# Hybrid streaming encoder step on one core: the residual rows' scaling and the first operand set of the lower product are put beside the second pair of up-projections

## The chip, the cores and the metric

One core of a Trainium2 chip runs the whole step as one program. The metric is device microseconds of that program. Five engines matter: TensorE (PE, with its weight loads as PEld), VectorE (DVE), ScalarE (ACT), GpSimd (POOL) and SyncE (SP), which issues the transfers. Each engine runs its own instructions strictly in the order in which they were written out, and waits by semaphores for the others' data.

## What is computed

The reference is one layer of an encoder over 640 tokens (512 prompt, 128 sample), width 1024: attention and a convolution branch, a merge, then a feed-forward part, a gated embedding and a norm. The part that the change touches is the feed-forward part:

```
x = x + (gate_a * attn_branch + gate_c * conv_branch) @ w_out
x = x + square(relu(rmsnorm(x, norm_ffn_g) @ w_ff_up)) @ w_ff_down     # 1024 -> 4096 -> 1024
x = x + sigmoid(rmsnorm(x, ple_norm_g) @ w_ple_gate) * (p_emb @ w_ple_proj)
```

The norm's factor r per token is not applied before the up-projection. With y = square(relu((x*g) @ w_up)) the product gives y*r*r, so the kernel multiplies the residual rows x by the row `vrow` = 1/(r*r) = mean(x*x) + eps instead, adds y @ w_down to that, and lets the later norms take the factor out. The eight residual rows (128 channels x 640 tokens each) must therefore have been multiplied by `vrow` before the first result of the lower product is added to them.

## The kernel before, in words

All products keep full precision by splitting every operand into a high and a low part (high by ACT, low = value - high by DVE or POOL) and adding three matmuls. The feed-forward products use a seven-product scheme on 2x2 blocks, so each operand is first turned into seven combinations.

- `up(n)`, n = 0..15, is one block of the up-projection: four operand tiles A, B, C, D are prepared from two weight slabs `raw_up{n}a/b` (sums `S` at L1854, L1858, L1862, L1865; high parts L1839; low parts L1846), then seven products M1, M5, M6, M3, M7, M2, M4 of 12 matmuls each (L1918) go in that order into the PSUM banks a, b, a, b, a, c, a. `times` appends every product to the list `chain`. Sums of banks are L1957 and L1940; relu and square are L1978 to L1984. For even n the sums S lie in PSUM, for odd n in SBUF, made by POOL.
- Two blocks, up(2c) and up(2c+1), make a pair; their squared results y lie in one buffer `staged[c]`. There is one slot "y" for it in the plan: the first square of a pair (Z12 of the even block, which also gives back bank b) takes the slot, and the last low part of `convert(c)` gives it back. There are five banks "q" for the products.
- `convert(c)` makes the seven operands of the lower product from `staged[c]`: three differences on POOL and one on DVE (L2079), seven high parts on ACT (L2047), six low parts on DVE and one on POOL (L2054, all named f).
- `down(c)` is the lower product: four groups j of weights (`raw_down`, L2114 to L2141), each seven products of 6 matmuls (L2185) whose results DVE adds to the residual rows (L2222).
- `start_row(m)`, m = 0..7, multiplies residual row m by `vrow` on POOL (L1817). The addition L2222 to row m waits for it.

The order on each engine is made before the launch by a planner (`Plan`): every step is given an engine, an estimated cost, the steps that it depends on and a due key; the planner repeatedly takes the step with the least start + 0.01 x key. Steps that are listed as dependencies only shape this order; on the chip an instruction waits for its data alone. Slots of weight pairs ("w", three), raw slabs ("r", three), banks and ring tiles are granted in that plan too. In the plan before, `start_row` has the keys T_0 + 20 + 2m and depends on `vrow`, and `convert(0)` the key T_0 + 17.8, ahead of the products of up(2) (T_0 + 22.8) and up(3) (T_0 + 34.2). T_0 is the due key of the first up-projection.

Of the kernel before, what the change touches and what calls it, by code (L numbers as in the profile page):

```python
# [62 lines left out]
SQ2, START, SQ3 = "POOL", "POOL", "POOL"  # L63
# [8 lines left out]
FAST = (0, 1, 2, 3, 4, 5, 6)  # L72
# [27 lines left out]
class Plan:  # L100
# [7 lines left out]
    def op(self, eng, cost, fn, deps, key, get="", put=""):  # L108
        if eng == "DVE2":
            eng, port = "DVE", True  # L110
        else:
            port = eng == "POOL"
        self.port.append(port and LOCK > 0)
        self.ops.append((eng, cost, fn, [d if isinstance(d, tuple) else (d, self.wait) for d in deps], key, get, put))
        return len(self.ops) - 1
# [53 lines left out]
def encoder_step_kernel(ctx: ExitStack, tc: tile.TileContext, a: dict, o: dict):  # L169
# [597 lines left out]
    for m in range(4):  # L767
        ps = product(f"qn{m}", blocks(slab(), range(6)), cq, ntaps=QN_TAPS[m])
        for j in range(2):
# [5 lines left out]
                op=ALU.mult,  # L775
# [132 lines left out]
    for j in range(4):  # L908
# [3 lines left out]
        for i in range(2):  # L912
            m = 2 * j + i
# [13 lines left out]
    op = plan.op  # L927
# [57 lines left out]
    for m in range(4):  # L985
# [21 lines left out]
        c = op("PE", 1.3, kn, ukd, -20 + m, get="p")  # L1007
# [6 lines left out]
    for t in range(4):  # L1014
# [18 lines left out]
        c = op("PE", 1.3, vn, uvd, -16 + t, get="p")  # L1033
# [28 lines left out]
    for g in range(2):  # L1062
        k_, wkb, wkd = slab_op(-19, raw_only=True)
        for ct in range(2):
# [21 lines left out]
            c = op("PE", 0.87, qn, wkd, -19, get=QB)  # L1086
# [353 lines left out]
    op = plan.op  # L1440
# [38 lines left out]
    def token_row(i, out, dep, key):  # L1479

        bx = {}

        def diagonal():
            bx["dg"] = ring(f"dg_{i}")
            nc.vector.tensor_tensor(
                out=bx["dg"].rearrange("p (t n) -> p t n", t=NT),
                in0=ident[:, None, :].to_broadcast([P, NT, P]),
                in1=one[i][:, :, None].to_broadcast([P, NT, P]),
                op=ALU.mult,
            )  # L1490

        def spread():
            bx["b"] = [qbank(f"psb_{i}{s}") for s in range(2)]
            for s in range(2):
                nc.tensor.matmul(bx["b"][s][:, :HT], ones, bx["dg"][:, s * HT : (s + 1) * HT], start=True, stop=True)
            plan.give(bx["dg"])

        def copy():
            t = out()
            for s in range(2):  # L1500
                nc.scalar.activation(t[:, s * HT : (s + 1) * HT], bx["b"][s][:, :HT], AF.Copy)
            plan.give(*bx["b"])

        d1 = op("DVE2", 0.73, diagonal, [dep], key, get="t")
        d2 = op("PE", 0.6, spread, [d1], key, get="qq", put="t")
        return op("ACT", 0.7, copy, [d2], key, put="qq")
# [39 lines left out]
    chain = []  # L1546
# [121 lines left out]
    grid, sq_done, xr_done, readers = {}, [], {}, {}  # L1668
# [130 lines left out]
    T_0 = 6.5 * 4  # L1799
# [11 lines left out]
    a3 = token_row("v", lambda: vrow, a2, T_0 + 10)  # L1811
    squared = op("DVE", 0.1, v_squared, [a2], T_0 + 20)
    started = []

    def start_row(m):
        def go():
            engines[START].tensor_tensor(out=x2[m], in0=x2[m], in1=vrow, op=ALU.mult)  # L1817

        started.append(
            op(START, 1.5 if START == "POOL" else 0.73, go, [a3, (started or [a3])[-1]] + readers[m], T_0 + 20 + 2 * m)  # L1820
        )

    for m in range(8):
        start_row(m)

    staged, opened = {}, {}

# [537 lines left out]
    key, fdone = T_0, {}  # L2365

    def ups(c, key):
        fdone[c] = up(2 * c, key) + up(2 * c + 1, key + T_UP)
# [1 line left out]
    ups(0, key)  # L2370
    key += 2 * T_UP
    for c in range(8):
        opnds = (convert if c in FAST else plain_convert)(c, key - 5 if c == 0 else key, fdone[c])
        if c < 7:
            ups(c + 1, key)
            key += 2 * T_UP
        used.clear()
        (down if c in FAST else plain_down)(c, key, opnds)
        key += T_DN if c in FAST else 26.0
# [414 lines left out]
```

## Time and profile before

| | |
|---|---|
| median of three runs | 1003.73 us (997.35, 1003.73, 1003.88) |
| the profiled execution | 998.67 us |
| its span, first to last instruction | 996.8 us |
| PE busy | 968.8 us (97%) |
| DVE busy | 797.5 us (80%) |
| ACT, POOL busy | 506.4 us (51%), 371.4 us (37%) |
| chain that ended last | PE 88%, DVE 8%, ACT 2% |

Times are microseconds from the span's start. A busy PE is not PE at its peak: at the lower granted clock a matmul lasts longer and still counts as busy. In a timeline, a row gives start, duration, engine, line, operation, result and operands, and in brackets how long the engine had been idle before it and who ended that.

### The profile page before, as it was taken

The page shows a single profiled execution, that of the slowest core. Times are in us where ns is not written, and L with a number is a line of the kernel's source. Part 1 is how long each engine was busy: PE and PEld are TensorE (multiplying, and loading weights), DVE is VectorE, ACT ScalarE, POOL GpSimd, SP SyncE. Part 2 cuts the span into 40 slices and gives each one's busy share as a digit, 9 for nine tenths or more (in the row PEclk, how much of TensorE's full clock was granted, in tenths as well). Part 3 has the DMA queues.
Part 4 walks back from the last instruction along what each step waited for, and adds up shares of the span by engine and source line. Part 5 has one row for each costly group of instructions (what it writes and reads, how often), then busy time and mean ns, then how long its engine had stood idle before and what let it go on. Part 6 is the DMA issues. An engine that isn't in the chain of part 4 may idle for free.

```text
span 996.8 us, 17051 instructions
## 1 busy us (share of the span) xinstructions
PE 968.8 (97%) x6576; PEld 935.2 (94%) x6576; DVE 797.5 (80%) x1415; ACT 506.4 (51%) x939; POOL 371.4 (37%) x270
## 2 busy tenths in 40 slices
PE   9999999999999899999998999999999999999995
PEld 8999989999999667799998999999999999999995
DVE  7596899995554887687779999999999999996445
ACT  7344644223443687635665455555555555645442
POOL 0354559322201443001239435354545454323111
PEclk9999999999999999999998899999999999999998
DMA  6329213312242433414221132322222222342203
GB/s 234 117 81 96 96 49 101 117 64 85 64 132 71 136 105 115 131 44 143 86 72 56 64 89 84 98 83 93 85 86 85 85 85 85 112 128 64 86 1 106
DMA packets 34705, 92.53 MB, mean 93 GB/s; under 512 B 8800, under 2 KB 11488, under 8 KB 34624
## 3 DMA queue, kind: packets, MB, share of 16 engines
q1 hardware_dynamic: 34480, 91.42, 30.5%
q8 instruction: 52, 0.85, 0.3%
q14 instruction: 29, 0.24, 0.1%
q10 hardware_dynamic: 144, 0.03, 0.0%
HBM read 86.12 MB, written 3.91 MB: 90 GB/s over the span
## 4 chain that ended last, share of the span: by engine, by line
PE 88%; DVE 8%; ACT 2%; issue 1%; DMA 1%; POOL 0%; SPq 0%; DVEq 0%; POOLq 0%; ACTq 0%
PE a L1918 11%; PE da L2185 9%; PE sa L342 6%; PE sc L342 6%; PE wo L1687 6%; PE b L1918 5%; PE db L2185 5%; PE pg L2481 3%; PE ao L1624 3%; PE co L342 3%; PE pd L2301 3%; PE c L1918 3%; PE glu_b L342 2%; PE glu_a L342 2%; PE dc L2185 2%; PE pg L2557 2%
## 5 line engine op out<-in xcount | busy, mean ns | idle before, releaser
L2141 POOL TENSOR_TENSOR lo_B<-raw_down,hi_B 128x768 fp32r<-128x768 f32 x28 | 51.8, 1850 | 44.5 <-PE da L2185 24.4
L485 DVE SCALAR_TENSOR_TENSOR cv<-uP,keep,cv 128x512 f32<-128x512 f32 x87 | 65.6, 754 | 2.4
L2222 DVE TENSOR_TENSOR x<-da,x 128x320 f32<-128x320 f32 x112 | 53.8, 485 | 3.1 <-PE da L2185 0.9
L510 POOL TENSOR_TENSOR acc<-acc,tap 128x640 f32<-128x640 f32 x30 | 49.2, 1639 | 10.1 <-ACT tap L502 8.7
L2185 PE MATMUL da<-f,hi_B 128*128 128x320 f32 x224 | 50.2, 310 | 0.0
L2185 PE MATMUL da<-f,hi_A 128*128 128x320 f32 x224 | 49.5, 307 | 0.0
L2185 PE MATMUL db<-f,hi_A 128*128 128x320 f32 x224 | 49.5, 307 | 0.0
L1714 POOL TENSOR_TENSOR ssum<-ssum,sq 128x640 f32<-128x640 f32 x7 | 11.1, 1592 | 90.5 <-ACT sq L1711 90.5
L2122 POOL TENSOR_TENSOR raw_down<-raw_down 128x256 f32<-128x256 f32 x28 | 21.4, 764 | 61.2 <-DVE S L2114 60.8
L2134 ACT ACTIVATE hi_B<-raw_down 128x768 fp32r<-128x768 f32 x28 | 23.8, 848 | 31.5 <-PE a L1918 13.3
L1687 PE MATMUL wo<-mgl,hi_wo 128*128 128x320 f32 x128 | 39.4, 308 | 0.0
L1687 PE MATMUL wo<-mgh,hi_wo 128*128 128x320 f32 x128 | 39.1, 305 | 0.0
L1687 PE MATMUL wo<-mgh,lo_wo 128*128 128x320 f32 x128 | 39.0, 305 | 0.0
L2185 PEld LDWEIGHTS da<-f,hi_B 128*128 128x128 f32 x224 | 36.9, 187 | 0.7 <-DVE x L2222 0.2
L2185 PEld LDWEIGHTS db<-f,hi_A 128*128 128x128 f32 x224 | 37.1, 187 | 0.0
L2185 PEld LDWEIGHTS da<-f,hi_A 128*128 128x128 f32 x224 | 37.1, 187 | 0.0
L2134 ACT ACTIVATE hi_A<-S 128x512 fp32r<-128x512 f32 (+1 forms) x56 | 26.8, 479 | 17.4 <-DVE S L2128 17.4
L2185 PE MATMUL da<-f,lo_A 128*128 128x320 f32 x112 | 34.4, 307 | 0.8 <-DVE lo_A L2141 0.7
L2185 PE MATMUL da<-f,lo_B 128*128 128x320 f32 x112 | 34.2, 305 | 0.0
L2185 PE MATMUL db<-f,lo_A 128*128 128x320 f32 x112 | 34.2, 305 | 0.0
L2054 POOL TENSOR_TENSOR f<-y,f 128x640 fp32r<-128x640 f32 x7 | 11.7, 1675 | 59.7 <-ACT f L2047 59.7
L485 DVE SCALAR_TENSOR_TENSOR cv<-uS,keep,cv 128x128 f32<-128x128 f32 x87 | 31.0, 356 | 3.2
(684 smaller groups left out, 3770.6 us busy)
## 6 DMA issues: line engine op xcount, KB each, us to landing
raw_down<-in_w_down_dram SPq DMA_DIRECT2D x32, 512.0 KB, 3.7
raw_w_gate<-in_w_gate_dram SPq DMA_DIRECT2D x16, 512.0 KB, 3.5
raw_cache_T<-in_cache_T_dram SPq DMA_DIRECT2D x8, 512.0 KB, 3.8
raw_cache_V<-in_cache_V_dram SPq DMA_DIRECT2D x8, 512.0 KB, 3.5
raw_wo<-in_w_out_dram SPq DMA_DIRECT2D x8, 512.0 KB, 3.6
raw_pg<-in_w_pg_dram SPq DMA_DIRECT2D x8, 512.0 KB, 3.6
raw_w_glu<-in_w_glu_dram SPq DMA_DIRECT2D x6, 512.0 KB, 4.4
raw_w_cq<-in_w_cq_dram SPq DMA_DIRECT2D x6, 512.0 KB, 3.7
```

The costliest lines, as they stand in the source:

```text
L342: nc.tensor.matmul(ps[:m, s, :HT], w_, x_[:, s * HT : (s + 1) * HT], start=st_, stop=sp)
L485: nc.vector.scalar_tensor_tensor(out=outs[i] if j == W - 1 else sums[i], in0=src, scalar=wj, in1=sums[i], op0=ALU.mult, op1=ALU.add,)
L510: nc.gpsimd.tensor_tensor(out=acc[:, 0, :], in0=acc[:, 0, :], in1=t, op=ALU.add)
L1624: nc.tensor.matmul(ps[:, :HT], w_, x_[:, halves_[s]], start=k == 0 and n == 0, stop=k == 3 and n == 2)
L1687: nc.tensor.matmul(bx[s][:, :HT], w_, x_[:, n_], start=k == 0 and j == 0, stop=k == 7 and j == 2)
L1918: nc.tensor.matmul(bx[bank][:, :HT], w_, x_, start=first and k == 0 and i == 0, stop=k == 3 and i == 2, skip_group_check=True,)
L2134: nc.scalar.activation(bx[tile][0][:, dst], src(), AF.Identity)
L2141: eng.tensor_tensor(out=l_, in0=src(), in1=h_.bitcast(F32), op=ALU.subtract)
L2185: nc.tensor.matmul(bx[bank][:, :HT], w_, x_, start=first and n == 0 and i == 0, stop=n == 1 and i == 2, skip_group_check=True,)
L2222: nc.vector.tensor_tensor(out=d, in0=bx[bank][:, :HT], in1=d, op=ALU.add)
L2301: nc.tensor.matmul(ps[:, :HT], w_, x_, start=b_ == 0 and q_ == 0, stop=b_ == 3 and q_ == 2)
L2481: nc.tensor.matmul(bx[s][:, :HT], w_, x_[:, n_], start=k == 0 and i == 0, stop=k == 7 and i == 2)
```

## The change

`start_row` gets a gate. Row m additionally depends, in the plan, on one product of the second pair: `chain[n_ + 5 + m]`, where `n_` is the length of `chain` before up(2) was added, so the gates are M2 and M4 of up(2) and then M1, M5, M6, M3, M7, M2 of up(3). Its key moves from T_0 + 20 + 2m to T_0 + 60 + 2m. The eight rows are no longer created right after `vrow` but after up(2) and up(3). `convert(0)` is created there too: its key moves from T_0 + 17.8 to T_0 + 45.6, and it additionally depends on `chain[n_ + 1]`, which is M5 of up(2). The other seven calls of the conversion keep their keys and dependencies.

```
-    def start_row(m):
+    def start_row(m, gate_):
...
         started.append(
-            op(START, 1.5 if START == "POOL" else 0.73, go, [a3, (started or [a3])[-1]] + readers[m], T_0 + 20 + 2 * m)
+            op(
+                START,
+                1.5 if START == "POOL" else 0.73,
+                go,
+                [a3, (started or [a3])[-1], gate_] + readers[m],
+                T_0 + 60 + 2 * m,
+            )
         )
-
-    for m in range(8):
-        start_row(m)
...
     for c in range(8):
-        opnds = (convert if c in FAST else plain_convert)(c, key - 5 if c == 0 else key, fdone[c])
+        if c:
+            opnds = (convert if c in FAST else plain_convert)(c, key, fdone[c])
         if c < 7:
+            n_ = len(chain)
             ups(c + 1, key)
             key += 2 * T_UP
+            if c == 0:
+
+                opnds = convert(c, key, fdone[c] + [chain[n_ + 1]])
+                for m in range(8):
+                    start_row(m, chain[n_ + 5 + m])
```

## Rows read from the trace of the kernel before

**Rows 1.** Stretches, all engines: the first feed-forward stretch and the first later cycle, columns named

```profile
core 0: us, PE busy (x) PEld busy (x) DVE busy (x) ACT busy (x) POOL busy (x), PEclk, DMA share, GB/s
503.00:588.35 85.35, 79.47 (x510) 76.86 (x509) 75.42 (x121) 43.73 (x90) 51.06 (x32) 0.94 0.24 75
588.35:637.23 48.88, 48.88 (x339) 48.70 (x338) 46.22 (x90) 26.77 (x54) 23.17 (x16) 1.00 0.28 87
```

**Rows 2.** The first of those stretches, matmuls of L1918, then of L2185

```profile
503.00:588.35 85.35, 54.63 (x338) 52.48 (x339) 0.94 0.24 75
...
503.00:588.35 85.35, 23.52 (x156) 22.69 (x156) 0.94 0.24 75
```

**Rows 3.** Stretches of ten microseconds inside the first stretch, same columns as rows 1

```profile
530.00:540.00 10.00, 10.00 (x71) 9.94 (x69) 8.88 (x9) 5.78 (x12) 10.00 (x6) 1.00 0.17 53
540.00:550.00 10.00, 6.04 (x25) 5.38 (x25) 10.00 (x8) 3.87 (x6) 10.00 (x6) 0.65 0.16 52
550.00:560.00 10.00, 8.91 (x48) 8.04 (x47) 8.44 (x15) 5.67 (x14) 1.26 (x2) 0.84 0.22 68
```

**Rows 4.** Timeline of PE: matmuls after a wait, and two at the lower clock

```profile
542.16 0.41 PE L1918 MATMUL a<-h2t34h,hi_D 128*128 128x320 f32 x1 [1.89 <-DVE y L1940]
...
543.48 0.47 PE L1918 MATMUL a<-h2t34l,hi_D 128*128 128x320 f32 x1
543.75 0.47 PE L1918 MATMUL a<-h2t34h,lo_D 128*128 128x320 f32 x1
...
547.62 0.63 PE L1918 MATMUL a<-h2b,lo_A 128*128 128x320 f32 x1 [2.07 <-DVE lo_A L1846]
```

**Rows 5.** Chain that ended last, in order of time: start, length, what

```profile
560.70 1.73 PE c L1918 x12
...
564.17 0.88 PE da L2185 x6
```

**Rows 6.** Timeline of POOL: the residual rows and what is queued behind them

```profile
526.37 6.62 POOL L1817 TENSOR_TENSOR x<-x,vrow 128x640 f32<-128x640 f32 x4
532.94 2.03 POOL L2079 TENSOR_TENSOR T<-y 128x640 f32<-128x640 f32 x1
534.93 4.13 POOL L1817 TENSOR_TENSOR x<-x,vrow 128x640 f32<-128x640 f32 x2
539.02 2.00 POOL L2079 TENSOR_TENSOR T<-y 128x640 f32<-128x640 f32 x1
...
548.66 1.86 POOL L1862 TENSOR_TENSOR raw_up3b<-raw_up3a,raw_up3b 128x512 f32<-128x512 f32 x1
```

**Rows 7.** Timeline of DVE, from block 1's last squares to block 2's first

```profile
529.27 0.68 DVE L1846 TENSOR_TENSOR lo_B<-S,hi_B 128x512 fp32r<-128x512 f32 x1
529.87 0.47 DVE L1984 TENSOR_TENSOR y<-c,y 128x320 f32<-128x320 f32 x1
...
532.11 1.42 DVE L1846 TENSOR_TENSOR lo_C<-raw_up2b,hi_C 128x512 fp32r<-128x512 f32 x1 [1.12 <-ACT hi_C L1839]
...
535.44 2.19 DVE L2054 TENSOR_TENSOR f<-y,f 128x640 fp32r<-128x640 f32 x1
...
541.62 0.48 DVE L1940 TENSOR_TENSOR y<-a,u 128x320 f32<-128x320 f32 x1
...
549.31 1.76 DVE L1846 TENSOR_TENSOR lo_A<-S,hi_A 128x512 fp32r<-128x512 f32 x1
...
551.73 0.81 DVE L2054 TENSOR_TENSOR f<-T,f 128x640 fp32r<-128x640 f32 x1
...
557.70 0.48 DVE L1984 TENSOR_TENSOR y<-b,y 128x320 f32<-128x320 f32 x1
```

**Rows 8.** The tile raw_up3b: its issue on SP's queue, and its transfer

```profile
L1526 SPq DMA_DIRECT2D raw_up3b<-in_w_up_dram x1: 328/328/328, 535.6 to 535.6; - x1
...
DMA to landing us min/median/max: 3.5/3.5/3.5
```

## The prediction, made before the changed kernel was run

> **What bounds the kernel now.** I read the page first: PE is busy nearly all the time, so only stretches in which PE is not at full pace can give anything. The stretches by time show where that is. From 588.35 us on the feed-forward part repeats in cycles of 48.88 us in which PE is busy for all of it at full clock [rows 1]; what is saved ahead of 588.35 therefore reaches the end, and what is lost there too. The stretch before it is the only slow one. A cycle has 339 matmuls in 48.88 us, 0.144 us each [rows 1]. The slow stretch holds 338 + 156 = 494 of them [rows 2], worth 71.2 us; the norm's sum and the spreading of `vrow` and the tail of the product before take about 2.4 us more (an estimate: 510 - 494 = 16 other PE instructions in [rows 1, 2]). It lasts 85.35 us. So **about 11.8 us are lost**, half as idle PE (85.35 - 79.47 = 5.9 us, [rows 1]) and half at the lower clock: in the two stretches from 540 to 560 the granted clock averages 0.65 and 0.84 [rows 3], and matmuls start 0.27 us apart instead of 0.144 [rows 4]. Of TensorE's two levels (2.4 and 1.2 GHz) that is the lower one; what came before the fall is a wait of 1.89 us for a sum of block 2 that DVE made late [rows 4].
>
> The timelines of DVE and POOL tell why. From 532.1 to 551.0 DVE never rests, and neither does POOL [rows 3, 6]. A DVE instruction with both operands in SBUF takes 0.81 us when POOL is idle (551.73), but 1.42 to 2.19 while POOL works; one with an operand in PSUM keeps its 0.47 to 0.68 us (529.27, 529.87, 541.62) [rows 7]. Ten instructions of the first kind, from 532.11 to 549.31, took 18.0 us together, **1.8 us each**, against 8.1 at 0.81, beside nine of POOL [rows 6, 7]: while POOL's queue is full, DVE gets through about one of them per POOL instruction.
>
> The Trainium skill (GPSIMD Engine Reference, section Specifications) says that GpSimd's SBUF interfaces are shared with VectorE and are contended by Vector instructions with two SBUF inputs. The trace agrees, with the 0.81 against 2.19 us above; the page speaks against moving eight more POOL instructions beside such work, which is the doubt weighed below.
>
> One hidden chain matters. Z12 of up(2) needs the slot "y" that the last low part of `convert(0)` gives back, and it gives back the bank that M2 of up(3) needs. Before, the last low part is at 551.73 and Z12 at 557.70 [rows 7], ending at 558.2; M2 of up(3) starts at 560.70 and the lower product at 564.17 [rows 5].
>
> **The change, part by part.**
>
> *Removed from POOL's queue ahead of the conversion:* eight rows. Four ran from 526.37 and two stood between the first and the second difference, 4.13 us [rows 6]. The first difference needs y of block 1, written by 530.34 [rows 7], and stood at 532.94: it can come 2.6 us earlier, the second about 4.1 + 2.6 = 6.7 us earlier. The plan's gate M5 of up(2) holds nothing on the chip, since it is no data dependency; it only fixes the place in the queues.
>
> *Moved in priority:* `convert(0)` now ranks behind the work of up(2) and up(3), so the late sum at 541.62 [rows 7] should no longer stand behind two conversions of 2.2 us each. That removes most of the 1.89 us wait and, I think, the fall of the clock behind it.
>
> *No transfer is added.* The slabs' order is the same. raw_up3b is issued at 535.6 and lands 3.5 us later [rows 8]; its buffer comes free with the second lo_C, at 535.5 before and about 1 us earlier without a row beside it, so POOL's sums for up(3) can start at about 538.3.
>
> *Added contention.* Count DVE's two-SBUF instructions until Z12. Before: ten slow and eight quick ones. After: POOL does its first two differences by 533.9 and is then idle until 538.3. In that gap DVE does about six quickly (lo_C, lo_D, four of the conversion). At 538.3 POOL starts three sums, a difference and a low part (five instructions, 9 us at 1.8), and the rows follow at once, since their gates lie at 540 to 552. DVE's other ten (six of up(3)'s preparation, the sum among them, s4, and three of the conversion) then go at POOL's pace: 10 x 1.8 = 18.0, so 538.3 + 18.0 + 0.5 = **556.8 us for Z12**, with M2 of up(3) right behind it, against 560.70. The gain is 560.7 - 556.8 = 3.9, say **4 us**, and the lower product starts at 560.2 instead of 564.2.
>
> *The rows themselves* (unknown: what a row costs DVE beside it). Lower bound: nothing, if only PSUM instructions run beside it, as in most of 526 to 533. Upper: 1.8 - 0.7 = 1.1 us each, for five rows before Z12 5.5 us. I took the upper in the sum above, since up(3)'s preparation lies in SBUF. With the lower bound the last five of the ten take 0.7 each: 538.3 + 9.0 + 3.5 + 0.5 = 551.3, a gain of 9.4 us. The additions of the lower product wait for the rows; row 0 is done by about 549 and row 7 by 538.3 + 13 x 1.8 = 561.7, two rows are needed per group of about 6 us from 560 on: no cost. If that cover is gone, an addition waits at most one row, 1.8 us, and holds bank a.
>
> *DVE's total is a limit of its own.* It is busy 75.4 of 85.35 us [rows 1], and the lower product's part is already near full on DVE, as in the later cycles with 46.2 of 48.9 [rows 1]. That is why I do not add the whole clock loss to the gain.
>
> **The rivals.**
>
> *Full success.* The rows meet only PSUM work, the clock stays up: 9.4 us up to all 11.8 us. For it: the rows at 526 to 533 cost DVE little. Against it: up(3) is the block whose sums lie in SBUF. Time 998.7 - 11 = 987.7.
>
> *No net change.* The same POOL and DVE work is only shifted: the contention leaves the first half of the second pair and comes back in the other. For it: DVE and POOL both full from 532 to 551 [rows 3, 6]. Time within 2 us of before: 998.7.
>
> *Slower.* The lower rank of `convert(0)` puts its last low part behind all of up(3)'s preparation and the first two of the lower product's: four more at POOL's pace, 4 x 1.8 = 7.2 us, Z12 at 564.0. M2 of up(3) then waits for its bank and the lower product starts 3.3 us later than before; PE's idle time comes in one piece and the lower clock with it, as before. Time 1002.0. It decides from the point where the last low part ends later than about 560. Against it: DVE has a free gap of 4 us early, and the plan gives the conversion its turn whenever up(3) waits for a weight slot.
>
> **How the numbers follow.** Chances: partial gain, 2 to 8 us: 0.47; full success: 0.18; no net change: 0.20; slower: 0.15. The sum is made against the profiled execution, 998.67: 998.7 - 4 = 994.7. The runs shown lie at 997.35 and twice at 1003.8, with the profiled one near the first; off the median of 1003.73 the same 4 us give 999.7. Nothing in the profile says which level the median of the next runs takes, so I forecast the middle, **997 us**. The likeliest case alone is 991 to 1002. The range goes from full success at the lower level (987) to the slower case between the levels (1005). About 1% (10 us) is what a measurement of this kernel can tell from no change. Faster by more than that needs full success, or a partial one together with a change of level: 0.22. Slower by more than that needs more than the slower rival gives: 0.08. Within 1%: 0.70.
>
> **What would show it.** Right: the first difference of the conversion at about 530.4 on POOL; the sum L1940 of block 2 no later than 540.4 and no wait near 2 us before M4 of up(2); rows L1817 only after about 545; low parts of up(3) still at 1.4 to 2.0 us beside them; M2 of up(3) at 556 to 557, the first L2185 near 560; cycles of 48.9 us afterwards. Wrong: low parts at 0.7 us beside the rows (then full success), or the last low part of the conversion after 560 with PE idle ahead of M2 of up(3) (then slower). The clock is the step I trust least: if it does not fall at all, the gain grows by up to 5.9 us; if it falls with a new wait, the gain goes.

## The result, and the profile after

| | before | after |
|---|---|---|
| median, us (runs on one chip) | 1002.63 (997.35 to 1004.75) | 1007.85 (999.65 to 1012.11) |
| ratio after/before, 95% interval | | 1.0058 (1.0039 to 1.0077) |
| profiled execution, us | 998.67 | 1009.14 |
| its span, us | 996.8 | 1007.3 |

One further run of the changed kernel, 2442.40 us, stands outside the range and the ratio.

The changed kernel is slower by 0.58%, some 5.8 us. Forecast were 997 us and a range up to 1005; the sign is that of the rival "slower", and the size is beyond it. The profiled execution of the kernel before is one of its quicker ones (998.67 us against a median of 1002.63), that of the changed kernel lies near its median. The two differ by 10.5 us: the stretches below show where the time goes, and show more of it than the 5.8 us of the ratio.

First the stretches of time. The feed-forward part reaches from the first up-product (503.10 us before, 504.20 after) to the first matmul of the plain lower product behind it (882.4 and 892.9). It took 379.3 us before, in this row of the kernel before (columns as in [rows 1]: length, then the busy time of PE, PEld, DVE, ACT and POOL, the granted clock, the DMA share and rate):

```profile
503.10:882.40 379.30, 373.42 (x2531) 369.58 (x2530) 353.96 (x656) 206.11 (x407) 184.25 (x124) 0.99 0.27 86
```

The same view of the changed kernel: the whole part, 10-us pieces of it, and a later cycle.

```profile
504.20:892.90 388.70, 375.68 (x2530) 372.37 (x2529) 351.21 (x655) 206.66 (x407) 182.43 (x124) 0.98 0.26 84
...
540.00:550.00 10.00, 6.78 (x45) 6.25 (x44) 9.65 (x8) 2.42 (x4) 9.63 (x7) 1.00 0.00 0
550.00:560.00 10.00, 7.84 (x41) 7.58 (x42) 6.53 (x14) 5.52 (x12) 2.40 (x3) 0.83 0.33 107
560.00:570.00 10.00, 6.43 (x34) 6.16 (x33) 7.16 (x13) 5.66 (x13) 9.63 (x6) 0.83 0.16 52
...
580.00:590.00 10.00, 8.15 (x45) 8.15 (x46) 8.28 (x17) 2.49 (x5) 6.77 (x5) 0.83 0.16 54
...
647.88:696.67 48.79, 48.79 (x339) 48.69 (x338) 45.08 (x90) 26.92 (x54) 22.79 (x16) 1.00 0.27 87
```

The part is 388.7 - 379.3 = 9.4 us longer. PE idles 388.70 - 375.68 = 13.0 us in place of 379.30 - 373.42 = 5.9, which is 7.1 us; the same matmuls, some 2530, take 375.68 - 373.42 = 2.3 us more, at the lower mean clock (0.98 against 0.99). In [rows 3] the clock fell once, to 0.65 and 0.84 between 540 and 560. Now it holds to 550 and is then at 0.83 in three pieces up to 590, and once more between 610 and 620 (0.83). The later cycle is as long as in [rows 1] (48.79 against 48.88), and so is all that follows it to the end of the part (245.03 us from 647.88 on, 245.16 before from 637.23 on): nothing is lost or won there.

Next, what PE waits for. The timeline of PE in the changed kernel, every matmul behind a wait between 536 and 640 (start, length, what, and in brackets the idle time and its releaser):

```profile
546.40 0.42 PE L1923 MATMUL b<-h2t12h,lo_A 128*128 128x320 f32 x1 [1.37 <-DVE lo_A L1851]
...
551.30 0.64 PE L1923 MATMUL a<-h2t12h,hi_B 128*128 128x320 f32 x1 [3.15 <-ACT y L1938]
...
559.18 0.41 PE L1923 MATMUL a<-h2t34h,hi_D 128*128 128x320 f32 x1 [0.86 <-DVE y L1945]
...
564.79 0.53 PE L1923 MATMUL c<-h2b2h,hi_C 128*128 128x320 f32 x1 [3.57 <-DVE y L1989]
...
581.85 0.53 PE L2190 MATMUL da<-f,lo_A 128*128 128x320 f32 x1 [2.08 <-DVE lo_A L2146]
...
614.74 0.41 PE L1923 MATMUL a<-h2t12h,hi_B 128*128 128x320 f32 x1 [1.82 <-ACT y L1938]
```

The six make 12.85 us, nearly all of the 13.0. (The rows, L1817 before, are L1819; all lines behind them have moved by five: the matmul L1918 is L1923, the late sum L1940 is L1945, Z12's sum L1984 is L1989, the lower product L2185 is L2190.) The wait of [rows 4] in front of M4 of up(2), 1.89 us for the late sum, is gone, and so is the 2.07 behind it. In their place stand waits in up(3), one of them for Z12's bank, one in the lower product, and one in the next pair.

POOL's timeline shows what the low rank does to its queue, and where the rows go.

```profile
531.54 1.57 POOL L2084 TENSOR_TENSOR T<-y 128x640 f32<-128x640 f32 x1 [5.40 <-PE a L1923]
538.68 1.53 POOL L1859 TENSOR_TENSOR S<-raw_up3b 128x512 f32<-128x512 f32 x1 [5.57 <-DMA raw_up3b<-in_w_up_dram]
...
544.26 1.54 POOL L2084 TENSOR_TENSOR T<-y 128x640 f32<-128x640 f32 x1
545.76 2.00 POOL L1819 TENSOR_TENSOR x<-x,vrow 128x640 f32<-128x640 f32 x1
547.73 1.98 POOL L2084 TENSOR_TENSOR T<-y,T 128x640 f32<-128x640 f32 x1
557.60 1.66 POOL L2059 TENSOR_TENSOR f<-y,f 128x640 fp32r<-128x640 f32 x1 [7.89 <-ACT f L2052]
...
579.42 2.09 POOL L2146 TENSOR_TENSOR lo_B<-raw_down,hi_B 128x768 fp32r<-128x768 f32 x1 [0.26 <-ACT hi_B L2139]
...
583.17 1.55 POOL L1819 TENSOR_TENSOR x<-x,vrow 128x640 f32<-128x640 f32 x1
```

The first difference stands at 531.54, where before it stood at 532.94 [rows 6]. Then POOL idles 5.57 us, not for want of work but because the next instruction of its queue, the first sum for up(3), waits for its transfer. The second difference is behind that sum and three more instructions, at 544.26 instead of 539.02. The last of the eight rows stands at 583.17: only two start ahead of 564, and six at 565.98 or later, around and in the lower product.

DVE does the low parts of the conversion late:

```profile
539.58 0.50 DVE L1945 TENSOR_TENSOR y<-a,u 128x320 f32<-128x320 f32 x1 [0.52 <-PE a L1923]
...
544.35 2.00 DVE L1851 TENSOR_TENSOR lo_A<-S,hi_A 128x512 fp32r<-128x512 f32 x1
546.27 2.04 DVE L1851 TENSOR_TENSOR lo_B<-S,hi_B 128x512 fp32r<-128x512 f32 x1
548.24 2.02 DVE L1870 TENSOR_TENSOR S<-raw_up3a,S 128x512 f32<-128x512 f32 x1
...
559.71 0.93 DVE L2059 TENSOR_TENSOR f<-T,f 128x640 fp32r<-128x640 f32 x1
...
563.33 1.01 DVE L2059 TENSOR_TENSOR f<-T,f 128x640 fp32r<-128x640 f32 x1
564.26 0.48 DVE L1989 TENSOR_TENSOR y<-b,y 128x320 f32<-128x320 f32 x1
...
580.17 1.62 DVE L2146 TENSOR_TENSOR lo_A<-raw_down,hi_A 128x256 fp32r<-128x256 f32 x1
```

The last low part of the conversion ends at 564.3 (551.73 + 0.81 = 552.5 in [rows 7]) and Z12 stands at 564.26 instead of 557.70. Two more things are to be seen. Three instructions in a row at 2.0 us (544.35 to 550.2) stand beside POOL's difference, row and difference; the third is the sum s4 of up(3). And in the lower product, at 580.17, a low part takes 1.62 us beside a low part of POOL (579.42 to 581.5), which began 0.26 us after a row had ended, when its high part came from ACT; where POOL leaves DVE's low part alone it takes 0.42. PE's wait of 2.08 us at 581.85 is for it.

ACT shows what the stretched s4 does, and what else stands in its queue:

```profile
550.29 0.63 ACT L1844 ACTIVATE hi_B<-S 128x512 fp32r<-128x512 f32 x1 [6.09 <-DVE S L1870]
550.83 0.42 ACT L1938 ACTIVATE y<-a 128x320 f32<-128x320 f32 x1
...
554.88 0.44 ACT L1938 ACTIVATE u<-a 128x320 f32<-128x320 f32 x1 [2.79 <-PE a L1923]
```

ACT idles 6.09 us for s4, and the copy that frees bank a, which has nothing to do with s4, is behind it in the queue. That is PE's wait of 3.15 us. At 554.88 ACT has idled 2.79 us more, for PE; the next high part of the conversion is behind that copy, at 555.22, though both of the differences still to be split had been written by 549.7. POOL's low part at 557.60 and the last three of DVE belong to high parts that ACT does from 555.22 to 560.5.

### The profile page after: what moved, and what is told of

The parts are those of the page before. It is cut to its first block, busy times and chain, and to the rows that moved or that the text cites. A ratio compares the mean times of both kernels' runs of the same rounds, so it can differ in the third digit from the quotient of the medians.

```text
span 1007.3 us, 17053 instructions
## 1 busy us (share of the span) xinstructions
PE 971.1 (96%) x6576; PEld 937.6 (93%) x6576; DVE 794.7 (79%) x1415; ACT 506.7 (50%) x939; POOL 369.6 (37%) x270
## 5 line engine op out<-in xcount | busy, mean ns | idle before, releaser
L2190 PE MATMUL db<-f,hi_A 128*128 128x320 f32 x224 | 49.9, 309 | 0.1
L2190 PE MATMUL da<-f,hi_A 128*128 128x320 f32 x224 | 50.1, 309 | 0.0
L2190 PE MATMUL da<-f,hi_B 128*128 128x320 f32 x224 | 50.0, 309 | 0.0
L2190 PEld LDWEIGHTS db<-f,hi_A 128*128 128x128 f32 x224 | 37.5, 190 | 0.4 <-issue 0.4
L2190 PEld LDWEIGHTS da<-f,hi_A 128*128 128x128 f32 x224 | 37.6, 190 | 0.0
L2190 PEld LDWEIGHTS da<-f,hi_B 128*128 128x128 f32 x224 | 37.0, 187 | 0.4
L2190 PE MATMUL da<-f,lo_A 128*128 128x320 f32 x112 | 34.7, 310 | 2.1 <-DVE lo_A L2146 2.1
L2139 ACT ACTIVATE hi_A<-S 128x512 fp32r<-128x512 f32 (+1 forms) x56 | 26.9, 481 | 18.5 <-DVE S L2133 18.5
L2139 ACT ACTIVATE hi_A<-raw_down 128x256 fp32r<-128x256 f32 x28 | 11.7, 418 | 47.4 <-PE db L2190 19.3
L2190 PE MATMUL db<-f,lo_A 128*128 128x320 f32 x112 | 34.3, 307 | 0.0
L2190 PE MATMUL da<-f,lo_B 128*128 128x320 f32 x112 | 34.2, 306 | 0.0
```

The source lines that it names most:

```text
L2139: nc.scalar.activation(bx[tile][0][:, dst], src(), AF.Identity)
L2190: nc.tensor.matmul(bx[bank][:, :HT], w_, x_, start=first and n == 0 and i == 0, stop=n == 1 and i == 2, skip_group_check=True,)
```

## Experiments

Four theories. **A**: the conversion's low rank does it; Z12's bank is late, so either part of the change apart would show that only the conversion costs. **B**: the rows do it; beside the second pair and the lower product they stretch DVE's work, and the conversion costs nothing. **C** and **D** are about how a row costs: **C**, by the traffic between SBUF and POOL that DVE meets; **D**, by the time that it fills in POOL's queue.

All ratios are against the kernel before in interleaved runs on the same chip. Beside them stands where the feed-forward part of the one profiled execution went: from its first up-product to the first matmul of the lower product, from there to the first up-product of the pair behind it, and the rest (the second border shifts by up to a dozen matmuls, 1.7 us at 0.144, with the order that the plan chooses). The start of the part itself lies between 503 and 509 us, by what came before it; so the sums of the three columns are compared, not the spans. A sum is one execution, with its own falls of the clock, and differs from what the ratio gives by up to 3.6 us: the columns tell where a kernel loses, the ratio how much.

| kernel | ratio (95%) | to lower product | lower product | rest | sum |
|---|---|---|---|---|---|
| before | 1 | 60.9 | 24.2 | 294.2 | 379.3 |
| after | 1.0058 (1.0039 to 1.0077) | 63.9 | 28.2 | 296.6 | 388.7 |
| rows late only | 1.0057 (1.0036 to 1.0079) | 56.1 | 30.7 | 297.6 | 384.3 |
| conversion late only | 1.0041 (1.0019 to 1.0063) | 65.2 | 24.2 | 294.7 | 384.2 |
| before, no rows | 0.9966 (0.9943 to 0.9988) | 54.6 | 25.0 | 294.7 | 374.2 |
| after, no rows | 1.0000 (0.9978 to 1.0022) | 60.9 | 24.2 | 294.0 | 379.1 |
| rows late only, rows replaced | 0.9989 (0.9967 to 1.0011) | 56.1 | 24.7 | 297.5 | 378.3 |
| after, other bank for M2 of up(3) | 1.0125 (1.0099 to 1.0151) | 70.5 | 27.4 | 293.8 | 391.8 |
| before, three rows on DVE | 0.9989 (0.9971 to 1.0007) | 62.0 | 23.8 | 294.5 | 380.3 |
| before, norm and rows earlier | 0.9982 (0.9962 to 1.0002) | 59.0 | 25.0 | 294.7 | 378.7 |
| after, differences early | 1.0059 (1.0037 to 1.0081) | 62.5 | 25.1 | 294.5 | 382.1 |
| both of the two "before, ..." edits | 1.0021 (1.0003 to 1.0039) | 56.9 | 26.4 | 296.0 | 379.2 |
| after, high and low parts early | 1.0076 (1.0054 to 1.0098) | 60.9 | 26.5 | 296.5 | 383.9 |

**Each half of the change alone.** Rows late, the conversion where it was (against the changed kernel):

```diff
     for c in range(8):
-        if c:
-            opnds = (convert if c in FAST else plain_convert)(c, key, fdone[c])
+        opnds = (convert if c in FAST else plain_convert)(c, key - 5 if c == 0 else key, fdone[c])
...
-                opnds = convert(c, key, fdone[c] + [chain[n_ + 1]])
                 for m in range(8):
                     start_row(m, chain[n_ + 5 + m])
```

> Only the rows get their gates and late keys; the conversion keeps its key T_0 + 17.8 and its place. Theory A (the loss comes from the conversion's lower rank: its last low part ended at 552.5 before and at 564.3 after, Z12 of up(2) follows it, and M2 of up(3) waited 3.6 us for the bank): no loss here, Z12 at or before 558, the time 0 to 6 us below the kernel before. Theory B (the loss comes from the rows, which now run on POOL beside the two-SBUF work of up(3) and of the lower product): slower than before by about 5 us, low parts of 1.4 to 2.0 us wherever a row runs.

Conversion late, the rows where they were (against the kernel before):

```diff
     for c in range(8):
-        opnds = (convert if c in FAST else plain_convert)(c, key - 5 if c == 0 else key, fdone[c])
+        if c:
+            opnds = (convert if c in FAST else plain_convert)(c, key, fdone[c])
         if c < 7:
+            n_ = len(chain)
             ups(c + 1, key)
             key += 2 * T_UP
+            if c == 0:
+                opnds = convert(c, key, fdone[c] + [chain[n_ + 1]])
```

> Only the conversion is moved (key T_0 + 45.6, gate M5 of up(2)); the rows stay right behind vrow as before. Theory A: slower than before by 5 us or more, Z12 of up(2) after 562 and PE idle for 3 us or more ahead of M2 of up(3). Theory B: within 2 us of before, since no row has moved.

Measured: 1.0057 and 1.0041. Both halves cost, and together they cost 0.58%, not 0.57 + 0.41 = 0.98%. (A had set 5 us or more for the second; 0.41% is 4.1.) Their places differ. Late rows shorten the way to the lower product from 60.9 to 56.1 us and lengthen the lower product from 24.2 to 30.7. The kernel with late rows alone, timeline of PE, its two longest waits:

```profile
552.58 0.54 PE L1923 MATMUL b<-h2t12h,lo_A 128*128 128x320 f32 x1 [2.95 <-DVE lo_A L1851]
...
585.93 0.42 PE L2190 MATMUL da<-f,lo_A 128*128 128x320 f32 x1 [2.70 <-DVE lo_A L2146]
```

its timeline of DVE ahead of the second one, four stretched instructions:

```profile
573.21 1.82 DVE L2119 TENSOR_TENSOR S<-raw_down 128x256 f32<-128x256 f32 x1
...
576.07 1.61 DVE L2146 TENSOR_TENSOR lo_A<-raw_down,hi_A 128x256 fp32r<-128x256 f32 x1
...
581.00 2.13 DVE L2084 TENSOR_TENSOR T<-y,T 128x640 f32<-128x640 f32 x1
...
583.86 2.02 DVE L2146 TENSOR_TENSOR lo_A<-raw_down,hi_A 128x256 fp32r<-128x256 f32 x1
```

and POOL's instructions beside these four:

```profile
573.17 1.56 POOL L1819 TENSOR_TENSOR x<-x,vrow 128x640 f32<-128x640 f32 x1
...
575.86 1.54 POOL L1819 TENSOR_TENSOR x<-x,vrow 128x640 f32<-128x640 f32 x1
...
580.89 1.56 POOL L2084 TENSOR_TENSOR T<-y 128x640 f32<-128x640 f32 x1
...
583.80 1.80 POOL L2146 TENSOR_TENSOR lo_B<-raw_down,hi_B 128x768 fp32r<-128x768 f32 x1 [1.34 <-ACT hi_B L2139]
```

Two of them stand beside a row, and two beside work of POOL's own that now coincides with DVE's; the low part that PE waits for, 2.02 us, is one of the latter. A late conversion does the reverse: 65.2 us to the lower product, and the lower product untouched at 24.2. The kernel with the late conversion alone, timeline of PE:

```profile
565.42 0.63 PE L1918 MATMUL c<-h2b2h,hi_C 128*128 128x320 f32 x1 [5.08 <-DVE y L1984]
```

That is the bank that Z12 gives back. So A and B are each half right, and neither is right alone.

**The same two places with no rows at all.** Both kernels leave the eight multiplications of the residual rows out; the rank of the conversion is that of before in the first and that of after in the second. The steps stay in the plan, on no engine and at no cost, so the planner also comes to another order of the other work:

```diff
         def go():
-            engines[START].tensor_tensor(out=x2[m], in0=x2[m], in1=vrow, op=ALU.mult)
+            pass
...
```

> The kernel before with the eight multiplications of the residual rows by vrow left out (the residual goes in unscaled), nothing else changed by hand. It prices the rows where they stood. Theory A: 2 to 5 us faster than before, because the first difference of the conversion no longer stands behind them. Theory B: 5 us or more faster, since the contention goes with them.

> The changed kernel with the same eight multiplications left out. Theory A: still 3 us or more slower than the kernel before, Z12 of up(2) still after 560. Theory B: at or below the kernel before, since what cost the time is gone.

Measured: 0.9966 and 1.0000. The second came out as B had it in time and as A had it in place: Z12 still after 560 (563.95). The late conversion costs 0.34% without rows too, and all of it in front of the lower product (54.6 to 60.9 us in these two executions). The second of the two, timeline of PE:

```profile
564.48 0.64 PE L1923 MATMUL c<-h2b2h,hi_C 128*128 128x320 f32 x1 [5.14 <-DVE y L1989]
```

The wait for Z12's bank is as long as with rows (5.08): it is the rank that makes it, not the rows. Why it reads only 3.57 in the changed kernel isn't settled: PE has lost 1.37 + 3.15 + 0.86 = 5.38 us ahead of it there, but 4.39 in the kernel with the late conversion alone too, which waits 5.08. The rows cost 0.34% where they were (1 - 0.9966), 0.58% in the changed kernel (1.0058 - 1.0000) and 0.91% in the kernel with late rows alone (1.0057 - 0.9966); each of the three has 0.2 to 0.3% either way, and holds what the rows do to the plan as well. By place, early rows cost 60.9 - 54.6 = 6.3 us ahead of the lower product and nothing in it (most of the 6.3 is the lower clock of [rows 3], which the execution without rows escaped: PE is busy 55.9 us of that stretch with them and 50.4 without); late rows cost 56.1 - 54.6 = 1.5 ahead of it and 30.7 - 25.0 = 5.7 in it, and 2.9 behind it. Late rows are dearer than early ones.

**What of a row costs.** The kernel with late rows alone, each row replaced by a POOL instruction on 128x7 numbers of a scratch tile (the residual stays without its factor):

```diff
         def go():
-            engines[START].tensor_tensor(out=x2[m], in0=x2[m], in1=vrow, op=ALU.mult)
+            s_ = cols_[:, 9:16]
+            nc.gpsimd.tensor_tensor(out=s_, in0=s_, in1=pw[:, 1:2].to_broadcast([P, 7]), op=ALU.pow)
...
```

> The order of the run with the rows alone moved, but each of the eight multiplications is replaced by a power of 128x7 elements on a small scratch tile: POOL should be held about as long (the 128x5 form took 1.18 us, the 128x3 form 0.79; estimate 1.57) while next to nothing is read from SBUF. The residual goes in unscaled. Theory C (rows cost by stretching DVE's two-SBUF instructions): back to the kernel before without rows, about 0.3% below the kernel before; the halved low parts L2146 at 0.42 us and the difference L2084 at 0.82 us beside them. Theory D (rows cost because other POOL work stands behind them in its queue): as with the rows alone moved, 0.5% above the kernel before.

The plan's cost of a row is unchanged, and by the two traces every engine runs the same instructions in the same order as in the kernel with late rows alone, so this pair differs in the row's operands and in nothing of the plan. The replacement lasts about as long as a row, 1.48 us (the 128x3 form of the expectation takes 0.98 in the kernel before, not 0.79). Its line, all eight (least, median and greatest in ns):

```profile
L1821 POOL TENSOR_TENSOR cols<-cols x8: 1467/1484/1940, 554.7 to 591.0; 128x7 f32<-128x7 f32 x8
```

The time is 0.9989 of before, against 1.0057 with the rows, and the lower product takes 24.7 us in place of 30.7. That is all of the difference between the two sums, 384.3 - 378.3 = 6.0. Of these, 3.7 are PE's idle time (30.69 - 25.72 against 24.72 - 23.48), and the rest is its busy time, at a granted clock of 0.94 in place of 1.00. The 297.5 us behind the lower product stay, so the row's operands don't make the 2.9 us there. Timeline of DVE in this kernel (its lines are two further on), the same four instructions of the lower product:

```profile
575.53 0.42 DVE L2121 TENSOR_TENSOR S<-raw_down 128x256 f32<-128x256 f32 x1
...
577.27 0.58 DVE L2148 TENSOR_TENSOR lo_A<-raw_down,hi_A 128x256 fp32r<-128x256 f32 x1
...
581.61 0.81 DVE L2086 TENSOR_TENSOR T<-y,T 128x640 f32<-128x640 f32 x1
...
583.35 0.92 DVE L2148 TENSOR_TENSOR lo_A<-raw_down,hi_A 128x256 fp32r<-128x256 f32 x1
```

From 1.82, 1.61, 2.13 and 2.02 they fall to 0.42, 0.58, 0.81 and 0.92, the first three beside a replaced row, the last in part beside a difference of POOL. Counted over the whole lower product: DVE's 24 instructions with both operands in SBUF take 19.2 us with late rows and 14.4 with the rows replaced; at the shortest duration of each shape here (0.41 us for 256 columns, 0.68 for 512, 0.81 for 640) they would take 12.3. So 6.9 us of stretching become 2.1; in the kernel before without rows it is 1.3. (Stretching isn't yet lost time: the kernel before has 2.9 us of it in its lower product and takes 24.2 there.) Theory C holds, and D doesn't: of the 0.91% that late rows cost, 0.68 (1.0057 - 0.9989) goes with the row's SBUF operands, and the remaining 0.23 (0.9989 - 0.9966) lies within the intervals of the two runs. One thing else is taken away with the operands, the wait of an addition of the lower product for its row; but with the rows, too, no instruction of DVE there waits for POOL, and PE's only wait that is put down to an addition was 0.35 us. The Trainium skill (GPSIMD Engine Reference, section Specifications) says that GpSimd shares its SBUF interfaces with VectorE, and that this is felt by Vector instructions with two SBUF inputs; these runs agree, and give the size: beside a row, 1.82 us for a sum of 128x256 that takes 0.42 beside an instruction as long on 128x7.

**Taking the wait for Z12's bank away.** In the changed kernel, M2 of up(3) takes its bank from those of the sums:

```diff
...
-        M2 = times(mul("c", "C", 512, "B21", give=["C"]), [wa12] + X["B21"], key + 8, "q", "w")
+        M2 = times(mul("c", "C", 512, "B21", give=["C"]), [wa12] + X["B21"], key + 8, "v" if n == 3 else "q", "w")
...
```

> The changed kernel, but bank c of up(3) is taken from the banks of the sums S instead of the products' five, so M2 of up(3) no longer waits for Z12 of up(2). If the bank is what held M2 (3.6 us of idle PE ahead of it), that wait goes, M2 follows M7 directly and the time falls by 2 to 4 us against the changed kernel, part of it given back where the lower product needs its first bank. If M2 waited for something else, the wait stays and the time is that of the changed kernel, 0.6% above the kernel before.

Measured: 1.0125, a miss. Timeline of PE:

```profile
551.87 0.42 PE L1923 MATMUL c<-h2b2h,lo_C 128*128 128x320 f32 x1 [4.33 <-DVE lo_C L1851]
...
575.52 0.90 PE L2190 MATMUL da<-f,hi_A 128*128 128x320 f32 x2 [6.07 <-DVE y L1989]
```

M2 no longer waits for Z12, but the plan now puts it where its low part isn't ready, and Z12, later still, holds the bank of the lower product instead, for 6.07 us. The wait for Z12's bank has moved to that bank's next user. The edit moves the order as well as the bank, so what the bank alone is worth stays open.

**Giving rank back by halves.** In the changed kernel, first the four differences alone at their old rank (27.8 earlier), then the high and low parts alone:

```diff
-        t1 = op(DN_T[0], ..., ready_, key, get="t")
+        t1 = op(DN_T[0], ..., ready_, key - (27.8 if c == 0 else 0), get="t")
...
```

> The changed kernel with the four differences of convert(0) alone given back their old rank (27.8 lower keys); its high and low parts keep the low rank. The second difference then stands right behind the first on POOL, as the prediction had assumed, instead of behind the sums of up(3). If POOL's order made the conversion late: Z12 of up(2) falls from 60 us after the first up-projection's start (564.3 - 504.2) to about 55, as before (557.7 - 503.1), M2 of up(3) no longer waits, 2 to 4 us faster than the changed kernel. If the low parts' place on DVE and ACT made it late: Z12 stays past 58 and the time stays within 2 us of the changed kernel.

```diff
         def spl(name, src, deps, key, new=False, give=(), more=(), last=False):
+            key -= 27.8 if c == 0 else 0
```

> The counterpart: the changed kernel with the high and low parts of convert(0) given back their old rank on ACT, DVE and POOL, and the four differences left at the low one. If DVE's and ACT's order made the conversion late, Z12 of up(2) comes back to about 55 us after the first up-projection's start and the wait of M2 goes; the time is then that of the run with the rows alone moved, 0.5% above the kernel before, or better. If POOL's order made it late, the wait of M2 stays at 3 us or more.

Measured: 1.0059 and 1.0076; neither takes the loss away. Timeline of POOL with the differences early:

```profile
534.35 3.10 POOL L2084 TENSOR_TENSOR T<-y 128x640 f32<-128x640 f32 x2 [5.42 <-PE a L1923]
```

Both differences now stand one behind the other, as the prediction had them, in the gap in which POOL had idled. Z12 still stands 58.6 us after the start of the part, against 60.1 in the changed kernel and 54.6 before: POOL's order made 1.5 us of the delay at most. With the high and low parts early Z12 is at 55.9, and no wait for its bank is left: their low rank made most of the delay, 4.2 of 5.5 us. The way to the lower product is back at 60.9 us, as before, and the ratio is that of the rows alone moved, within the intervals (1.0076 and 1.0057); the lower product and the rest, 26.5 and 296.5, stay above those of before, as with late rows alone. Ahead of the lower product PE now waits elsewhere. Timeline of PE:

```profile
560.62 0.41 PE L1923 MATMUL a<-h2t34h,hi_D 128*128 128x320 f32 x1 [2.87 <-DVE y L1945]
...
564.26 0.64 PE L1923 MATMUL a<-h2t34h,lo_D 128*128 128x320 f32 x1 [3.08 <-DVE lo_D L1851]
```

One reading is that DVE has the same instructions to do in the same stretch, and PE waits for whichever it does last; no run here tests that by itself.

**Looking for a better place of the rows.** In the kernel before: rows 5 to 7 on DVE; then the norm's sum, mean and spreading with a due key lower by 6, so that all eight rows come ahead of the first difference; then both.

```diff
-            engines[START].tensor_tensor(out=x2[m], in0=x2[m], in1=vrow, op=ALU.mult)
+            engines["DVE2" if m > 4 else "POOL"].tensor_tensor(out=x2[m], in0=x2[m], in1=vrow, op=ALU.mult)
...
```

> The kernel before with rows 0 to 4 on POOL as they were and rows 5 to 7 on DVE right behind vrow, none of them later than the first difference of the conversion. If the rows cost their 4 us mainly by standing ahead of and between the conversion's differences, this gains 1 to 3 us; if it is their total work that costs, DVE pays for three rows at about 1.8 us each beside POOL and nothing is gained.

```diff
-    a1 = op("PE", 0.6, r2_sum, [sq_done[-1]], T_0 + 10, get="q")
-    a2 = op("DVE", 0.1, r2_mean, [a1], T_0 + 10, put="q")
-    a3 = token_row("v", lambda: vrow, a2, T_0 + 10)
+    a1 = op("PE", 0.6, r2_sum, [sq_done[-1]], T_0 + 4, get="q")
+    a2 = op("DVE", 0.1, r2_mean, [a1], T_0 + 4, put="q")
+    a3 = token_row("v", lambda: vrow, a2, T_0 + 4)
```

> The kernel before with the norm's sum, mean and spreading given the key T_0 + 4 instead of T_0 + 10, so that vrow comes earlier and all eight rows stand ahead of the conversion's first difference on POOL. If the place of the rows decides, 1 to 4 us faster (the bound is the kernel without rows, 0.34% below). If the rows now stretch the preparation of up(1) instead, no gain.

The third kernel has both edits and no other:

> The kernel before with vrow earlier (key T_0 + 4) and rows 5 to 7 on DVE, so that POOL has five rows only, all ahead of the conversion. If POOL's two-SBUF work between 532 and 551 is what costs, 2 to 4 us faster than the kernel before, near the bound of the kernel without rows (0.34% below). If DVE's own three rows at about 1.8 us each delay the preparation of up(1) or up(2), no faster than the kernel before.

Measured: 0.9989, 0.9982 and 1.0021. In the first the planner put DVE's third row at 548.53, behind both of POOL's first differences (537.24 to 540.8) and not ahead of them, so that run doesn't test the place that was meant. With the norm earlier, POOL's timeline reads:

```profile
518.29 11.50 POOL L1817 TENSOR_TENSOR x<-x,vrow 128x640 f32<-128x640 f32 x6 [0.94 <-ACT vrow L1501]
```

Counted from the start of the part, the rows begin at 11.6 us; before it was 18.5, with two rows at 521.61 ahead of those of [rows 6]. Six run in a row, and the other two (534.17) stand ahead of the first difference (537.23) as well. It is the best version with all of the work in it, and its interval holds 1: a gain of 0.2% at the most likely, not shown. The two edits together don't add, they are slower than before if anything (1.0003 to 1.0039); no version found here clearly beats the kernel before.

## Why the prediction was wrong, step by step

**First difference at 530.4, rows after 545, late sum by 540.4, no wait in front of M4 of up(2): these came true.** Measured were 531.54 (the part starts 1.1 us later), 545.76, 539.58, and no wait at 542. The low parts beside POOL took 2.0 us (forecast 1.4 to 2.0), and the cycle afterwards 48.8.

**"In that gap DVE does about six quickly (lo_C, lo_D, four of the conversion)", and Z12 at 556.8: this step failed.** It read the lower rank as "behind up(2) and up(3)" where that was welcome, and otherwise left the queues in order of data. But the rank holds on each engine. On POOL it put the second difference behind up(3)'s sums, whose transfer wasn't there, and POOL idled 5.57 us; "POOL does its first two differences by 533.9" failed with that, though the operands were there, as the run with early differences shows, which does both behind each other. That run also shows that this alone didn't cost the time (1.0059). On ACT and DVE the rank put the high and low parts behind the work of up(3): DVE did two of the conversion's instructions in the quick gap, not four, and took up the rest at 541.8, 552.6, 559.7, 562.3 and 563.3. With these parts at their old rank Z12 comes back from 60.1 to 55.9 us after the start of the part. The late conversion by itself costs 0.41%, and 0.34% without rows.

The sum had a second flaw. It let M2 of up(3) follow Z12 and took the 3.9 us between 560.70 and 556.8 as the gain. In the kernel before, M2 didn't wait for Z12, which had ended 2.5 us earlier (558.2, [rows 5, 7]); what PE had lost ahead of M2 was its own waits, 1.89 + 2.07 + 0.84 + 0.25 us, and the lower clock. The gain at the lower product was there all the same where the conversion kept its rank: with late rows alone the way to it is 4.8 us shorter in the profiled executions, and the lower product then takes 6.5 us longer. (A smaller slip: of the ten undisturbed instructions put at 8.1 us, five are 128x512 at 0.68, so 7.5.)

**The rival "slower" had the place and the wait, and its 564.0 is luck in part.** It let M2 of up(3) wait for its bank (3.57 us at 564.79), and put Z12 at 564.0 us (measured 564.26). It got there by four more low parts at POOL's pace of 1.8 us. Measured, POOL idled 7.89 us ahead of its low part at 557.60, and DVE's low parts from 552.6 on took 0.81 to 1.01 us; the last three of them couldn't start before ACT's high parts, which stood behind a copy that waited 2.79 us for PE. Its ground for the low chance was the free gap on DVE and the plan's turns for the conversion; neither got the conversion done. What the way to the lower product cost is 63.9 - 60.9 = 3.0 us, near the rival's 3.3: idle PE grew by (1.37 + 3.15 + 0.86 + 3.57) - (1.89 + 2.07 + 0.84 + 0.25) = 3.9 us, and 0.9 came back in PE's busy time (55.9 to 54.9 us), at a mean clock of 0.95 against 0.92 over that stretch.

**"The rows beside the lower product: no cost": this term failed too.** Of the 9.4 us by which the two profiled executions differ in this part, 6.4 came behind the start of the lower product (28.2 - 24.2, and 296.6 - 294.2). The sum had row 7 done by 561.7, with five rows ahead of Z12; it was done at 584.7, with two ahead of Z12 and the others around and in the lower product. The step looked only at whether a row is done when its addition comes, and no addition is seen to wait for one. It did not ask what a row does to the DVE instructions beside it there, though the same prediction had priced that at up to 1.1 us each in up(3). Without rows the changed kernel's lower product takes 24.2 us; the rows cost it 4.0. DVE's two-SBUF instructions there are stretched by 4.6 us in all in the changed kernel, counted as above, and by 1.8 without rows. Late rows by themselves cost 5.7 to 6.0 us there, and the run with the replaced rows shows that this goes with their operands in SBUF. How the 0.58% divides between the two failed steps isn't settled: each half by itself costs more than half of it.

**"It is only shifted" was right for DVE's sum.** DVE is busy 351.21 us against 353.96 before, so its work hardly changed; PE waits for another part of it. The other bank and the two halves of the rank each moved a wait without winning the time back.

**The gain by the clock.** The prediction took the 1.89 us wait for the cause of the fall and let the clock stay when that wait went. The wait went; the clock held until 550 and fell then, behind waits of 1.37 and 3.15 us. That a wait of this size can be followed by a fall and needn't be is told below.

**Why both halves do not add.** Late rows free POOL and DVE early, 4.8 us by the lower product (60.9 to 56.1), and the late conversion gives that up again (63.9): part of the two prices is paid once. Why the changed kernel's lower product takes 28.2 us and not the 30.7 of late rows alone isn't settled; one reading is that only four of its eight rows run after the lower product has begun (568.05), against six with late rows alone, the last at its very end; no run here separates that.

## What to carry to other kernels

A lower rank for one chain holds on every engine's queue: look, engine by engine, at what comes to stand in front of the moved work and whether that waits for a transfer or a slow sum. Work that a deadline allows to be late isn't free where it runs: price it by what it does to the instructions beside it on the other engine, and here that price was higher in the new place (0.91%, the conversion left where it was) than in the old (0.34%). To tell an engine's time from its memory traffic, replace the instruction by one as long that touches almost no memory.

## What the runs showed of the hardware

The same waits of PE were not followed by the same granted clock. Three kernels here have the same three waits in up(3) and just ahead of it, 0.73, about 0.4 and 2.95 us. The kernel before without rows kept its clock behind them: its wait, in the timeline of PE,

```profile
551.15 0.41 PE L1918 MATMUL b<-h2t12h,lo_A 128*128 128x320 f32 x1 [2.95 <-DVE lo_A L1846]
```

and the two 10-us pieces around it:

```profile
540.00:550.00 10.00, 7.01 (x43) 5.96 (x41) 9.01 (x10) 6.36 (x12) 7.84 (x5) 1.00 0.15 56
550.00:560.00 10.00, 8.85 (x61) 8.85 (x62) 8.34 (x16) 5.10 (x12) 1.84 (x3) 1.00 0.35 107
```

The kernel with late rows alone, which waits 2.95 us at 552.58, shows a fall in the second of these pieces and another one later (in the third kernel, that with the rows replaced, the clock is 0.83 from 550 to 560 too):

```profile
550.00:560.00 10.00, 7.42 (x40) 7.43 (x41) 9.57 (x14) 5.18 (x11) 5.22 (x5) 0.83 0.23 70
580.00:590.00 10.00, 7.30 (x41) 7.03 (x40) 9.03 (x14) 2.25 (x5) 4.41 (x4) 0.84 0.33 103
```

Executions of one kernel differ in the same way. The changed kernel took 999.65 us at a mean granted clock of 0.995 and 1012.11 at 0.984; the kernel before 997.31 at 0.994 and 1005.26 at 0.983. So most of the scatter of a kernel, 8 to 12 us, goes with its mean granted clock in that execution, and it is as large as the largest effect measured here: one profile can't be read for a half per cent, only the ratios can.
